# Row scales from squared rows of x, two projection pairs run alternately, and gate weights prepared early, in one hybrid mixer layer

## The chip, the cores and the metric

The kernel runs on one core of one Trainium2 chip. The metric is device time of one execution, in microseconds (us). The core's engines each work through their own instructions in order: TensorE (PE in the profile), VectorE (DVE), ScalarE (ACT), GpSimd (POOL) and SyncE (SP, which issues the DMAs). [...]

## The reference, cut to what matters

One layer, with 2048 tokens and 1024 channels. `w_in` has 8200 columns: q, k, v, the output gate, z_m, the i and f gates (4 columns each), u, B, C and z_c.

```python
h    = rms_norm(x, g_pre)                    # x * rsqrt(mean(x*x) + eps) * g_pre, per token
proj = einsum('bsd,de->bse', h, w_in)
q, k, v, o, z_m, i_pre, f_pre, u, gate_b, gate_c, z_c = split(proj)
hm   = mlstm_chunkwise(q*scale, k, v, i_pre + b_i, log_sigmoid(f_pre + b_f))   # 4 heads
y_m  = silu(z_m) * sigmoid(o) * group_rms_norm(hm, g_head, 4)
conv = causal_depthwise_conv(gate_c * u, conv_w)                               # 3 taps
y_c  = silu(z_c) * group_rms_norm(gate_b * conv, g_conv, 16)
out  = einsum('bse,ed->bsd', concat(y_m, y_c), w_out)
return x + rms_norm(out, g_post)
```

## The kernel before, in words

**Matmuls.** The inputs are float32, and PE multiplies in a rounded float32 format. So every operand is split into a rounded high part and the rest, its low part: a cast on ACT and a subtraction on DVE (`split_h`, `split_l`, L187 to L195). A product is then three matmuls per 128 rows of contraction: high by high, high by low, low by high (`mm_prod`, L300).

**Pairs and products.** The tokens are in two halves of 1024, each in two quarters of 512. The output columns of the projection are in 32 pairs of 128-column blocks (`PAIRS`). For one half of the tokens, a pair is a 2 by 2 block product (two column blocks, two token quarters, the contraction in two halves). It is done in the manner of Strassen and Winograd with 7 products instead of 8 (`pair`, L502). Each product is 12 matmuls of 512 columns into one of three banks of PSUM, X, D and Y. Between products the banks are copied or added on ACT and DVE (`evac`, L513): Y starts as a copy of X (L516), then p is copied from D (L519) and u2 from Y (L522). The token operands of the 7 products (hH and hL) are made once for a half, in seven sets j. The weight operands (w) are made for each product, some slots ahead (`plan_weights`, L294).

**Slots.** A slot is one product. An agenda (`on`, `later`, `run_slot`) holds what each slot emits behind its matmuls, sorted by level: evacuations, weights, stores, the rest. The order in which the program is written this way is kept on each engine (`in_order`), so nothing is reordered later. What falls into one slot stands in a row on its engine.

**The passes.** The opening (`start`, L918) loads x transposed, normalises the first half of the tokens, and does pairs 0 and 1 without Strassen, from operands that are not yet divided by the row's norm (uH, uL). The results are multiplied by the row's scale afterwards (`plain`, `plain_take`). Then come pairs 2 to 31 of the first half, 32 pairs of the second half, and two passes of the output projection with 16 pairs of 7 products each. Beside the pairs the agenda runs the gates (`plan_gates`), 32 groups of two chunks of mLSTM (`plan_group`, 16 for each half of the tokens), the convolution, and in the last pass the closing row norms (`row_take`, `row_rstd`, `row_out`).

**The opening's row scales.** ACT squares the 16 tiles of x transposed (L955). POOL adds them up over the channels (L960), a matmul by ones sums over the partitions and leaves the sum in every partition (`sum_up`, L964). ACT takes the root (L967) and DVE the reciprocal (L970): rb holds the scale of each token, in all partitions. With rb, `norm` scales x in place (L975), `diff` and `fill` make the 7 operand sets, and `plain_take` (L1017) scales the results of pairs 0 and 1. The gate projection (`gate_proj`, L558) takes weights wgt that `gate_weights` (L543) builds: a fill with zeros on DVE, two small casts on ACT, two small subtractions on DVE.

## Time and profile before

| | us |
|---|---|
| three runs, median (lowest to highest) | 1707.27 (1705.94 to 1707.9) |
| the profiled execution, its own time | 1707.94 |
| its span in the profile | 1706.2 |
| PE busy | 1653.8 (97%) |
| DVE busy | 1291.8 (76%) |
| ACT busy | 887.9 (52%) |
| POOL busy | 139.6 (8%) |

The mean granted clock of TensorE over the span is 0.987 of full speed. Below, a row of waits sums the idle time of an engine ahead of the instructions of one line, with the engine and line that ended it. A row of a timeline is one instruction, or several alike in a row ("x4", with their joint duration). Its bracket holds the engine's idle time just ahead of it and what ended that. Matmuls overlap in the pipeline, so their spacing, not their duration, is what each takes of PE's time.

### The profile page before, as it was taken

To read this page: it belongs to the slowest core of one execution; us is meant where nothing else is said; L and a number is where in the kernel's file an instruction comes from. 1 tells how busy PE (TensorE), PEld (TensorE's weight loads), DVE (VectorE), ACT (ScalarE), POOL (GpSimd) and SP (SyncE) were. 2 spreads that over 40 slices of the span, in tenths; PEclk is the share of its full clock that TensorE was granted. 3 is DMA by queue.
4 is the path that set the end of the run, shared out by engine and by line. 5 is a ranking of instruction groups with operands and counts; after the bars stand their busy time and mean duration, and the time that the engine had idled before them with its cause. 6 is when DMAs were issued, how large, how long until landed. Compare 5 with 4: busy or idle time off the path is not lost. (4 is left out here: it accounts for less than half of the span.)

```text
span 1706.2 us, 23384 instructions
## 1 busy us (share of the span) xinstructions
PE 1653.8 (97%) x7533; PEld 1368.6 (80%) x7533; DVE 1291.8 (76%) x2375; ACT 887.9 (52%) x1697; POOL 139.6 (8%) x152
## 2 busy tenths in 40 slices
PE   6789999999999999999999999999999999999997
PEld 4578888788888888778888888888888878887885
DVE  7887668788888798856556878686866685568886
ACT  6243446655655665634454556555655563355442
POOL 5000001010202000000000101010200000000110
PEclk9889999999999999999999999999999999999999
DMA  4177774546454788856876565556587788899774
GB/s 157 51 186 189 187 186 156 181 133 209 124 168 131 236 260 262 286 140 163 220 192 170 151 190 155 175 151 177 158 235 243 238 254 264 258 302 296 232 234 155
DMA packets 413389, 335.06 MB, mean 196 GB/s; under 512 B 191209, under 2 KB 305905, under 8 KB 413266
## 3 DMA queue, kind: packets, MB, share of 16 engines
q1 hardware_dynamic: 413266, 333.56, 66.0%
q8 instruction: 59, 0.97, 0.2%
q14 instruction: 64, 0.52, 0.1%
HBM read 214.71 MB, written 118.76 MB: 195 GB/s over the span
## 5 line engine op out<-in xcount | busy, mean ns | idle before, releaser
L188 ACT CAST w<-wraw 128x512 fp32r<-128x512 f32 x506 | 313.8, 622 | 278.6 <-PE uY L307 105.9
L191 DVE TENSOR_TENSOR w<-wraw,w 128x512 fp32r<-128x512 f32 x506 | 345.8, 686 | 120.0 <-ACT w L188 116.9
L305 PE MATMUL uY<-hH,w 128*128 128x512 f32 x936 | 368.3, 393 | 11.9 <-ACT uY L516 5.7
L306 PE MATMUL uY<-hL,w 128*128 128x512 f32 x936 | 365.7, 391 | 0.5 <-DVE hL L191 0.5
L307 PE MATMUL uY<-hH,w 128*128 128x512 f32 x936 | 366.2, 391 | 0.0
L305 PE MATMUL uX<-hH,w 128*128 128x512 f32 x624 | 245.5, 393 | 5.0 <-ACT w L188 5.0
L307 PE MATMUL uX<-hH,w 128*128 128x512 f32 x624 | 244.4, 392 | 4.2 <-DVE w L191 4.2
L305 PE MATMUL uD<-hH,w 128*128 128x512 f32 x624 | 244.5, 392 | 0.0
L306 PE MATMUL uX<-hL,w 128*128 128x512 f32 x624 | 244.0, 391 | 0.0
L307 PE MATMUL uD<-hH,w 128*128 128x512 f32 x624 | 243.6, 390 | 0.0
L306 PE MATMUL uD<-hL,w 128*128 128x512 f32 x624 | 243.3, 390 | 0.0
L305 PEld LDWEIGHTS uY<-hH,w 128*128 128x128 f32 x936 | 176.4, 188 | 51.2 <-ACT uY L516 7.5
L307 PEld LDWEIGHTS uY<-hH,w 128*128 128x128 f32 x936 | 176.2, 188 | 37.5
L306 PEld LDWEIGHTS uY<-hL,w 128*128 128x128 f32 x936 | 176.5, 189 | 36.6 <-DVE hL L191 1.1
L307 PEld LDWEIGHTS uX<-hH,w 128*128 128x128 f32 x624 | 117.7, 189 | 29.9 <-DVE w L191 4.9
L305 PEld LDWEIGHTS uX<-hH,w 128*128 128x128 f32 x624 | 117.8, 189 | 29.2 <-ACT w L188 5.5
L307 PEld LDWEIGHTS uD<-hH,w 128*128 128x128 f32 x624 | 117.2, 188 | 25.0
L306 PEld LDWEIGHTS uX<-hL,w 128*128 128x128 f32 x624 | 117.9, 189 | 24.0
L306 PEld LDWEIGHTS uD<-hL,w 128*128 128x128 f32 x624 | 117.4, 188 | 23.8
L305 PEld LDWEIGHTS uD<-hH,w 128*128 128x128 f32 x624 | 117.4, 188 | 23.5
L527 DVE TENSOR_TENSOR c<-p,uY 128x512 f32<-128x512 f32 x78 | 53.5, 686 | 93.0 <-PE uY L307 85.6
L421 POOL TENSOR_SCALAR hss<-hss 128x2 f32<-128x2 f32 x32 | 15.0, 470 | 1124.8 <-ACT num L790 1124.8
(198 smaller groups left out, 2275.7 us busy)
## 6 DMA issues: line engine op xcount, KB each, us to landing
wraw<-in_wt_dram SPq DMA_DIRECT2D x226, 256.0 KB
wraw<-w_scr SPq DMA_DIRECT2D x120, 256.0 KB
w_scr<-wraw SPq DMA_DIRECT2D x90, 256.0 KB
v_scr<-tr SPq DMA_DIRECT2D x128, 64.0 KB
vraw<-v_scr SPq DMA_DIRECT2D x32, 256.0 KB
h_scr<-hT SPq DMA_DIRECT2D x128, 64.0 KB
y_scr<-sg SPq DMA_DIRECT2D x32, 256.0 KB
g_scr<-c SPq DMA_DIRECT2D x32, 256.0 KB
```

The costliest lines, as they stand in the source:

```text
L188: nc.scalar.copy(dH, src)
L191: nc.vector.tensor_tensor(dL, src, dH.bitcast(F32), ALU.subtract)
L305: nc.tensor.matmul(bank, wH[:, k, :], bH[:, k, :], start=first, stop=False, **kw)
L306: nc.tensor.matmul(bank, wH[:, k, :], bL[:, k, :], start=False, stop=False, **kw)
L307: nc.tensor.matmul(bank, wL[:, k, :], bH[:, k, :], start=False, stop=stop and k == KH - 1, **kw)
L421: nc.gpsimd.tensor_scalar(t, t, scale, EPS, ALU.mult, ALU.add)
L527: nc.vector.tensor_tensor(c, sb["p"], bank["Y"], ALU.add)
```

## The change

**Row scales of the first half.** x is also loaded by rows (8 tiles of 128 tokens by 1024 channels, 512 KB each; `rows_load`). ACT squares a row tile and adds up along the row in the same instruction (`squares`, with accum_out). POOL turns four sums into four scales (`inverse`, by `rstd`: scale and eps, then the power -0.5, on 128x4). ACT multiplies the identity by each scale (`diagonal`), a matmul by ones spreads the diagonal over all partitions (`spread`), and ACT copies it to rb (`spread_take`). The squares of the transposed tiles, POOL's additions, ACT's roots and DVE's reciprocals are gone.

**Opening, other parts.** The gate weights' zero fill stands among the constants, and their load and splits stand ahead of the first slot's end. PE multiplies ones by zeros 16 times (128x128) before its first projection matmul. The two banks of pair 0's first quarter are copied to SBUF. The opening's steps stand in another order, set 1 is filled in the last slots ahead of pair 2, and sets 2, 4, 5 and 6 in the slots of pairs 2 and 3.

**Pairs 2 and 3.** Their 14 products run alternately (`two_pairs`, in the order TWO), pair 2's and 3's D banks in PSUM's pool "n".

**Groups, gates, last pass.** `plan_group` starts at slot 47 and every 10.4 slots (41 and 11 before), in the second half at U + 36 and every 10.8 (U + 34 and 11.3; U is the number of slots of a half). Within a group, q's scaling stands one slot later and in place, and its cast and subtraction one slot later. The steps of `plan_gates` from the row loads on stand one slot later, the takes of v of the opening 8 slots later. In the last pass `row_rstd` follows the second square at once instead of a slot later, and ot has 4 buffers instead of 5. The weights' raw tiles have 9 instead of 8.

The first place is ACT's order in the opening, from the end of the casts of pair 0's weights. Before (xs is x transposed, xsq its squares, w the weight operands, wgt the gate weights):

```order
L188 CAST w<-wraw 128x512 x2
L955 ACTIVATE xsq<-xs 128x512 x8
L188 CAST w<-wraw 128x512 x2
L947 ACTIVATE uH_172<-xs,gp 128x512 x4
L947 ACTIVATE uH_174<-xs,gp 128x512 x4
L967 ACTIVATE rb_167<-ssq,eps 128x512
L955 ACTIVATE xsq<-xs 128x512 x8
L188 CAST hH_430<-xs 128x1024 x2
L549 CAST wgt<-wgraw 128x8x4 x2
L564 COPY graw<-gate 100x512
```

After (xrows is x by rows, rs its sums of squares, dg the diagonal, graw the gate projection's result):

```order
L190 CAST w<-wraw 128x512 x4
L564 CAST wgt<-wgraw 128x8x4 x2
L1044 COPY u<-u 128x512 x2
L980 ACTIVATE xrows,rs_131<-xrows 128x1024 x4
L964 ACTIVATE uH_174<-xs,gp 128x512 x2
L989 ACTIVATE dg<-ident,rs_131 128x128 x4
L964 ACTIVATE uH_174<-xs,gp 128x512 x2
L964 ACTIVATE uH_176<-xs,gp 128x512 x4
L997 COPY rb_169<-ssq 128x512
L579 COPY graw<-gate 100x512
L980 ACTIVATE xrows,rs_131<-xrows 128x1024 x4
L989 ACTIVATE dg<-ident,rs_131 128x128 x4
```

The 16 squares of transposed tiles gave way to 8 squares of rows, four ahead of the second quarter's uH and four behind the first gate result. The gate weights' casts moved ahead of all of them.

The second place is ACT's order from the cast of a weight operand, ahead of and in pair 2. Before, pair 2 stands alone, and the hH in these rows are sets 5 and 6:

```order
L188 CAST w<-wraw 128x512
L188 CAST hH_676<-xs 128x1024 x2
L188 CAST w<-s_670 128x512
L188 CAST hH_688<-xs 128x1024
L188 CAST hH_688<-xs 128x512 x2
L188 CAST w<-wraw 128x512 x3
L516 COPY uY<-uX 128x512
L188 CAST w<-wraw 128x512
L519 COPY p<-uD 128x512
L188 CAST w<-wraw 128x512
L522 COPY u_811<-uY 128x512
```

After, in the slots of pairs 2 and 3, where cs, p and u are evacuations of both (hH_787 is set 4, hH_840 set 5, and u_859 is pair 2's u2):

```order
L190 CAST w<-wraw 128x512
L190 CAST hH_787<-xs 128x1024
L323 COPY cs<-uX 128x512
L190 CAST w<-wraw 128x512
L190 CAST hH_787<-xs 128x1024
L524 COPY p<-uD 128x512
L190 CAST w<-wraw 128x512
L190 CAST hH_840<-xs 128x1024
L527 COPY u_859<-uY 128x512
L190 CAST w<-wraw 128x512
L190 CAST hH_840<-xs 128x1024
```

Casts of sets 4 and 5 now stand between the evacuations.

The third place is the end of DVE's order, the last row tiles of the output (ot the row, oss its sums of squares, xr the rows of x). Before:

```order
L461 TENSOR_TENSOR ot<-uY,pc 128x512
L474 TENSOR_TENSOR ot<-ot,gpost 128x512 x2
L485 TENSOR_TENSOR oss<-oss 128x1
L493 SCALAR_TENSOR_TENSOR ot<-ot,oss,xr 128x512 x2
L474 TENSOR_TENSOR ot<-ot,gpost 128x512
L485 TENSOR_TENSOR oss<-oss 128x1
L493 SCALAR_TENSOR_TENSOR ot<-ot,oss,xr 128x512 x2
```

After:

```order
L465 TENSOR_TENSOR ot<-uY,pc 128x512
L489 TENSOR_TENSOR oss<-oss 128x1
L478 TENSOR_TENSOR ot<-ot,gpost 128x512 x2
L489 TENSOR_TENSOR oss<-oss 128x1
L497 SCALAR_TENSOR_TENSOR ot<-ot,oss,xr 128x512 x2
L478 TENSOR_TENSOR ot<-ot,gpost 128x512
L497 SCALAR_TENSOR_TENSOR ot<-ot,oss,xr 128x512 x2
```

The first sum moved ahead of two products by gpost. The second moved ahead of the first tile's two output instructions and of the last product by gpost, and with each sum the power on POOL that follows it.

The core of the diff:

```diff
+    rs0 = const.tile([P, NC], F32, name="rs0")
     wgt = const.tile([P, KT, GW], F32R, name="wgt")
+    nc.vector.tensor_copy(wgt.rearrange("p k f -> p (k f)"), zero[:, 0:1].broadcast_to([P, KT * GW]))
...
-    rawp = ctx.enter_context(tc.tile_pool(name="rawp", bufs=8))
+    rawp = ctx.enter_context(tc.tile_pool(name="rawp", bufs=9))
...
-    wseq = [(hf, n, j) for hf in range(2) for n in range(NPAIR) if (hf, n) not in ((0, 0), (0, 1))
-            for j in range(NPROD)]
+    TWO = [(0, 2 + c, j) for c, j in (
+        (0, 0), (1, 0), (0, 3), (1, 3), (0, 1), (0, 2), (1, 1), (0, 4), (1, 2), (0, 5), (1, 4), (0, 6), (1, 5), (1, 6))]
+    wseq = TWO + [(hf, n, j) for hf in range(2) for n in range(NPAIR) if hf or n > 3 for j in range(NPROD)]
...
-        o = S["ot", t, qd] = op.tile([P, Q], F32, tag="ot", name="ot", bufs=5)
+        o = S["ot", t, qd] = op.tile([P, Q], F32, tag="ot", name="ot", bufs=4)
...
-                later(0 if last else 1, lambda: row_rstd(t, last))
+                row_rstd(t, last)
...
-    def pair(hf, n):
-        bank = {"X": bank_("uX"), "D": bank_("uD")}
+    def products(hf, n, d_bank):
...
+        def step(j):
+            if j < 2:
+                bank["XD"[j]] = (bank_, d_bank)[j]("u" + "XD"[j])
+            mm_prod(bank["XDYXYDY"[j]], wops.pop((hf, n, j)), hops[hf, j], j < 2, True)
+            later(1, lambda: evac(j), EVAC)
+            run_slot()
+
+        return step
...
+    def two_pairs():
+        steps = {n: products(0, n, lambda name: ps.tile([P, Q], F32, tag="n", name=name, bufs=2)) for n in (2, 3)}
+        for _, n, j in TWO:
+            steps[n](j)
...
     def gate_weights():
-        raw = sm.tile([P, KT, 8], F32, tag="wgraw", name="wgraw", bufs=1)
-        nc.sync.dma_start(raw, wg)
-        nc.vector.tensor_copy(
-            wgt.rearrange("p k f -> p (k f)"), zero[:, 0:1].broadcast_to([P, KT * GW]))
+        raw = S.pop("wg")
...
-            st["tq"] = ml.tile([P, 2, P], F32, tag="tmp", name="tmp")
+            st["tq"] = q
             nc.vector.tensor_tensor(
                 st["kT"], st["kT"], st["R"][:, :, P - 1 : P].broadcast_to([P, 2, P]), ALU.mult)
-            nc.vector.scalar_tensor_tensor(st["tq"], q, SCALE, st["iw"], ALU.mult, ALU.mult)
...
             nc.vector.scalar_tensor_tensor(st["R"], st["sT"], SCALE, st["R"], ALU.mult, ALU.mult)
+            nc.vector.scalar_tensor_tensor(st["tq"], st["tq"], SCALE, st["iw"], ALU.mult, ALU.mult)
             high("k")
-            high("q")
...
         def lows():
             high("p")
+            high("q")
             low("k")
+
+        def more_lows():
+            low("p")
             low("q")
...
-        def unscaled(b, k):
+        def u_high(b, k):
+            nc.scalar.activation(U[b][0][:, k], raw(b, k)[:, 0], AF.Copy, scale=col(b, k))
+
+        def u_low(b, k):
...
-        ssq, acc = {}, {}
-
-        def square(b, k):
-            sq = t5("xsq")
-            nc.scalar.activation(sq, raw(b, k)[:, 0], AF.Square)
-            qd = b % 2
-            if qd not in acc:
-                acc[qd] = sq
-            else:
-                nc.gpsimd.tensor_tensor(acc[qd], acc[qd], sq, ALU.add)
-
-        def sum_up(qd):
+        xt_, ssq, dg = {}, {}, {}
+
+        def rows_load(i):
+            if i % 2 == 0:
+                xt_[i // 2] = hop_tile(i // 4, "HL"[i // 2 % 2], "xrows", F32)
+            nc.sync.dma_start(flat(xt_[i // 2])[:, i % 2 * DM : i % 2 * DM + DM], x[i * P : (i + 1) * P, :])
+
+        def squares(i):
+            t = flat(xt_[i // 2])[:, i % 2 * DM : i % 2 * DM + DM]
+            nc.scalar.activation(t, t, AF.Square, accum_out=rs0[:, i : i + 1])
+
+        def inverse(qd):
+            rstd(rs0[:, 4 * qd : 4 * qd + 4], 1.0 / DM)
+
+        def diagonal(qd):
+            dg[qd] = t5("dg")
+            for i in range(4):
+                c = 4 * qd + i
+                nc.scalar.activation(
+                    dg[qd][:, i * P : (i + 1) * P], ident, AF.Copy, scale=rs0[:, c : c + 1])
+
+        def spread(qd):
             ssq[qd] = ps.tile([P, Q], F32, tag="g", name="ssq")
-            nc.tensor.matmul(ssq[qd], ones, acc[qd], start=True, stop=True)
-
-        def root(qd):
-            nc.scalar.activation(rb[:, seg(qd)], ssq[qd], AF.Sqrt, bias=eps, scale=1.0 / DM)
-
-        def inverse(qd):
-            nc.vector.reciprocal(rb[:, seg(qd)], rb[:, seg(qd)])
+            nc.tensor.matmul(ssq[qd], ones, dg[qd], start=True, stop=True)
+
+        def spread_take(qd):
+            nc.scalar.copy(rb[:, seg(qd)], ssq[qd])
...
+        def fill(j, b, which=slice(None)):
+            if (0, j) not in hops:
+                hops[0, j] = hop_tile(j, "H", f"hH{j}"), hop_tile(j, "L", f"hL{j}")
+            H, L = hops[0, j]
+            for k, n in parts(b)[which]:
                 split(H[:, k : k + n], L[:, k : k + n], raw(b, k, n))
...
+        def plain_copy(bank):
             t = t5("u")
+            nc.scalar.copy(t, bank)
+            return t
...
-            slow = NSTART + 2 * ch + qd - clock[0] if kind == "v" else 0
+            slow = NSTART + 8 + 2 * ch + qd - clock[0] if kind == "v" else 0
...
+        S["wg"] = sm.tile([P, KT, 8], F32, tag="wgraw", name="wgraw", bufs=1)
+        nc.sync.dma_start(S["wg"], wg)
+        for i in range(4):
+            rows_load(i)
...
+        for i in range(4, NC):
+            rows_load(i)
...
+        warm = ps.tile([P, 2, P], F32, tag="s", name="warm")
+        for _ in range(16):
+            nc.tensor.matmul(warm[:, 0, :], ones, zero, start=True, stop=True)
...
-        weights(1, 0)
-        weights(1, 1)
-        for half in range(2):
-            for k in range(KH):
-                square(2 * half, k)
-        weights(1, 2)
-        weights(1, 3)
-        run_slot()
-        for b in (1, 3):
-            for k in range(KH):
-                unscaled(b, k)
-        p1 = [plain(1, 0, 0, lambda: sum_up(0))]
-        root(0)
+        for q in range(4):
+            weights(1, q)
+        gate_weights()
+        copies = [plain_copy(banks[ch]) for ch in range(2)]
+        for i in range(4):
+            squares(i)
         inverse(0)
-        norm(0)
-        for b in (1, 3):
-            for k in range(KH):
-                square(b, k)
-        run_slot()
-        p1.append(plain(1, 1, 0))
+        run_slot()
+
+        p1 = [plain(1, ch, 0) for ch in range(2)]
+        u_high(1, 0)
...
+        spread(0)
+        spread_take(0)
+        run_slot()
+
+        gate = gate_proj(((U[0], 0), (U[2], 1)))
...
+        gate_take(0, 0, gate)
+        norm(0)
+        for i in range(4, NC):
+            squares(i)
+        inverse(1)
...
+        diagonal(1)
+        fill(0, 0)
+        run_slot()
+
+        p0.append(plain(0, 1, 1))
+        spread(1)
+        fill(3, 2)
+        spread_take(1)
+        run_slot()
+
+        nc.sync.dma_start(r_scr.rearrange("(o t) -> o t", o=1), rb[0:1, :])
+        p1 = [plain(1, 0, 1)]
+        norm(1)
...
+        diff(0, 1, 0)
+        run_slot()
+
         gate = gate_proj(((U[1], 0), (U[3], 1)))
-        run_slot()
...
+        run_slot()
+        on(clock[0], lambda: fill(1, 1))
+        on(clock[0], lambda: gate_take(0, 1, gate))
+        run_slot()
+        on(clock[0], lambda: diff(1, 3, 0))
+        run_slot()
+        on(NSTART + 2, lambda: diff(2, 2, 1))
+        for i, (j, b, at) in enumerate(((2, 1, 0), (4, 0, 3), (5, 2, 5), (6, 3, 7))):
+            on(NSTART + at, lambda j=j, b=b: fill(j, b, slice(0, 1)))
+            on(NSTART + at + 1, lambda j=j, b=b: fill(j, b, slice(1, None)))
...
-    plan_gates(0, 15, True)
+    plan_gates(0, 18, True)
     plan_gates(1, U + 9, False)
     for i in range(NH * NG):
         h, g = divmod(i, NG)
-        plan_group(0, h, g, 41 + 11 * i)
-        plan_group(1, h, g, U + 34 + int(11.3 * i))
+        plan_group(0, h, g, 47 + int(10.4 * i))
+        plan_group(1, h, g, U + 36 + int(10.8 * i))
...
-    for n in range(2, NPAIR):
+    two_pairs()
+    for n in range(4, NPAIR):
```

## Rows read from the trace of the kernel before

**Rows 1.** The page's first part: busy us (share of span) xinstructions.
```profile
PE 1653.8 (97%) x7533; PEld 1368.6 (80%) x7533; DVE 1291.8 (76%) x2375; ACT 887.9 (52%) x1697; POOL 139.6 (8%) x152
```

**Rows 2.** Waits of PE, whole span: line waiting <- engine, line waited for: us, times, longest.
```profile
PE gate L558 <- DVE wgt L550: 8.9, 1, 8.9
PE u L1002 <- ACT w L188: 6.4, 1, 6.4
PE uY L305 <- ACT uY L516: 5.7, 4, 2.0
PE uX L305 <- ACT w L188: 5.0, 1, 5.0
PE uX L307 <- DVE w L191: 4.2, 1, 4.2
PE ssq L964 <- POOL xsq L960: 3.9, 1, 3.9
```

**Rows 3.** Windows: length, busy us per engine, granted clock, DMA share, GB/s.
```profile
80.00:100.00 20.00, 10.82 (x33) 7.82 (x32) 19.36 (x25) 13.14 (x19) 0.00 (x0) 0.66 0.46 133
...
300.00:310.00 10.00, 7.98 (x30) 6.31 (x29) 9.72 (x19) 7.58 (x14) 2.05 (x2) 0.83 0.48 178
```

**Rows 4.** Timeline of PE: start us, us, line, op, [idle before <-releaser].
```profile
47.65 0.75 PE L558 MATMUL gate<-uH,wgt 128*100 128x512 f32 x1 [8.89 <-DVE wgt L550]
...
53.63 1.02 PE L964 MATMUL ssq<-xsq,ones 128*128 128x512 f32 x2
...
54.72 0.40 PE L1003 MATMUL u<-uL,w 128*128 128x512 f32 x1
...
76.72 0.39 PE L558 MATMUL gate<-uH,wgt 128*100 128x512 f32 x1
...
85.59 0.79 PE L305 MATMUL uX<-hH,w 128*128 128x512 f32 x1 [5.02 <-ACT w L188]
```

**Rows 5.** DMA rate in 40 slices of 0 to 100 us.
```profile
GB/s 18 193 379 370 394 380 388 379 39 0 3 0 0 7 0 0 96 114 0 0 0 0 0 3 11 95 220 0 0 7 0 149 169 107 116 105 0 215 331 22
```

**Rows 6.** Timeline of DVE in the opening.
```profile
30.56 3.34 DVE L970 RECIPROCAL rb<-rb 128x512 f32<-128x512 f32 x1
33.93 6.47 DVE L975 SCALAR_TENSOR_TENSOR xs<-xs,gp,rb 128x512 f32<-128x512 f32 x4
...
41.52 2.72 DVE L975 SCALAR_TENSOR_TENSOR xs<-xs,gp,rb 128x512 f32<-128x512 f32 x4
44.17 2.35 DVE L191 TENSOR_TENSOR hL<-xs,hH 128x1024 fp32r<-128x1024 f32 x2
```

**Rows 7.** Timeline of ACT in the opening.
```profile
14.76 4.28 ACT L955 ACTIVATE xsq<-xs 128x512 f32<-128x512 f32 x8
...
19.97 5.01 ACT L947 ACTIVATE uH<-xs,gp 128x512 fp32r<-128x512 f32 x8
...
81.14 3.88 ACT L188 CAST hH<-xs 128x1024 fp32r<-128x1024 f32 x4
...
112.61 0.59 ACT L319 COPY cs<-uY 128x512 f32<-128x512 f32 x1 [2.10 <-PE uY L307]
...
131.65 0.59 ACT L319 COPY cs<-uY 128x512 f32<-128x512 f32 x1 [2.06 <-PE uY L307]
```

**Rows 8.** POOL by line: ns min/median/max, of the whole span.
```profile
L960 POOL TENSOR_TENSOR xsq<-xsq x14: 1282/1593/1632, 16.0 to 39.9; 128x512 f32<-128x512 f32 x14
...
L422 POOL TENSOR_TENSOR rs<-rs,mhalf x1: 1635/1635/1635, 466.9 to 466.9; 128x8 f32<-128x8 f32 x1
```

**Rows 9.** Timeline of ACT near 300 us.
```profile
293.68 1.06 ACT L822 ACTIVATE xn<-xn 128x1024 f32<-128x1024 f32 x1
...
301.33 1.28 ACT L343 ACT_TABLE_LOAD   x1
```

**Rows 10.** Timeline of DVE at the end.
```profile
1696.16 1.29 DVE L474 TENSOR_TENSOR ot<-ot,gpost 128x512 f32<-128x512 f32 x2 [0.84 <-ACT junk L465]
...
1701.62 1.41 DVE L493 SCALAR_TENSOR_TENSOR ot<-ot,oss,xr 128x512 f32<-128x512 f32 x2 [1.01 <-POOL oss L422]
```

More of the change, by code (lines that the diff above doesn't have):

```diff
@@ L500, in bank_ @@
         return pps.tile([P, Q], F32, tag="pp", name=name)
-    def pair(hf, n):
-        bank = {"X": bank_("uX"), "D": bank_("uD")}
+    def products(hf, n, d_bank):
+        bank = {}
         sb = {}
@@ L534, in evac, with pair @@
                 take(0, 1, bank["Y"], True)
-        for j in range(NPROD):
-            b = bank["XDYXYDY"[j]]
-            mm_prod(b, wops.pop((hf, n, j)), hops[hf, j], j < 2, True)
-            later(1, lambda j=j: evac(j), EVAC)
-            run_slot()
+        def step(j):
[5 more added lines that the diff above has]
+        return step
+    def pair(hf, n):
+        step = products(hf, n, bank_)
+        for j in range(NPROD):
+            step(j)
+    def two_pairs():
+        steps = {n: products(0, n, lambda name: ps.tile([P, Q], F32, tag="n", name=name, bufs=2)) for n in (2, 3)}
+        for _, n, j in TWO:
+            steps[n](j)
     def gate_weights():
-        raw = sm.tile([P, KT, 8], F32, tag="wgraw", name="wgraw", bufs=1)
-        nc.sync.dma_start(raw, wg)
-        nc.vector.tensor_copy(
-            wgt.rearrange("p k f -> p (k f)"), zero[:, 0:1].broadcast_to([P, KT * GW]))
+        raw = S.pop("wg")
         for w in range(2):
@@ L982, in diff @@
                 sub(raw(o, k, n), raw(a, k, n), raw(b, k, n))
-        def fill(j, b):
-            H, L = hops[0, j] = hop_tile(j, "H", f"hH{j}"), hop_tile(j, "L", f"hL{j}")
-            for k, n in parts(b):
+        def fill(j, b, which=slice(None)):
[3 more added lines that the diff above has]
+            for k, n in parts(b)[which]:
                 split(H[:, k : k + n], L[:, k : k + n], raw(b, k, n))
@@ L1004, in plain_k, with plain @@
             nc.tensor.matmul(bank, wL[:, k, :], bH[:, k, :], start=False, stop=end)
-        def plain(n, ch, qd, between=None):
+        def plain(n, ch, qd):
             bank = bank_("u")
@@ L1010, in plain, with plain_take @@
                     plain_k(bank, n, ch, qd, half, k)
-                if half == 0 and between:
-                    between()
             return bank
-        def plain_take(n, ch, qd, bank):
+        def plain_copy(bank):
             t = t5("u")
+            nc.scalar.copy(t, bank)
+            return t
+        def plain_take(n, ch, qd, bank, t=None):
+            t = t or t5("u")
             nc.vector.tensor_tensor(t, bank, rb[:, seg(qd)], ALU.mult)
             kind, i = PAIRS[n]
-            slow = NSTART + 2 * ch + qd - clock[0] if kind == "v" else 0
+            slow = NSTART + 8 + 2 * ch + qd - clock[0] if kind == "v" else 0
             later(slow, lambda: TAKE[kind](0, i, ch, qd, t, False))
@@ L1044, in start @@
             for k in range(KH):
-                unscaled(2 * half, k)
+                u_high(2 * half, k)
+                u_low(2 * half, k)
                 if k == 0:
@@ L1069, in start @@
-        run_slot()
-        p1.append(plain(1, 1, 0))
-        for ch in range(2):
-            plain_take(0, ch, 0, banks[ch])
-        norm(2)
-        fill(0, 0)
-        gate_weights()
+        for q in range(4):
[4 more added lines that the diff above has]
+            squares(i)
+        inverse(0)
+        run_slot()
+        p1 = [plain(1, ch, 0) for ch in range(2)]
+        u_high(1, 0)
+        u_high(1, 1)
@@ L1076, in start @@
+        diagonal(0)
+        u_high(1, 2)
+        u_high(1, 3)
+        for k in range(KH):
+            u_low(1, k)
+            u_high(3, k)
+            u_low(3, k)
+        spread(0)
+        spread_take(0)
         run_slot()
         gate = gate_proj(((U[0], 0), (U[2], 1)))
-        sum_up(1)
+        for ch in range(2):
+            plain_take(0, ch, 0, copies[ch], copies[ch])
+        for ch in range(2):
+            plain_take(1, ch, 0, p1[ch])
         gate_take(0, 0, gate)
-        root(1)
+        norm(0)
@@ L1086, in start @@
-        for ch in range(2):
-            plain_take(1, ch, 0, p1[ch])
         norm(3)
         run_slot()
-        p0.append(plain(0, 1, 1))
-        diff(0, 1, 0)
-        diff(1, 3, 1)
-        fill(1, 1)
-        run_slot()
-        p1 = [plain(1, 0, 1)]
-        fill(3, 2)
-        diff(1, 3, 0)
+        p1.append(plain(1, 1, 1))
         for ch in range(2):
```

21 lines of the change are left out of this document (6 added, 15 removed).

## The prediction

> **What bounds the kernel now.** The profile's first part comes first. PE is busy for 1653.8 us of a span of 1706.2, so some 52 us are all that waits can hold; DVE at 76% comes next [rows 1]. The waits of PE come second. Five of them, all in the opening, are 8.9, 6.4, 5.0, 4.2 and 3.9, together 28.4 [rows 2]. Later waits are small: behind the copy uY four times, 5.7 in all, 2.0 at most [rows 2].
>
> The windows show what a wait costs beside its idle time: from 80 to 100 us the granted clock was 0.66, from 300 to 310 it was 0.83 [rows 3]. [...]
>
> The opening in one sum: the last copy of pair 3 starts at 131.65 [rows 7]. Up to there PE has 224 projection and gate matmuls, 51.9 us at 0.2316, two ssq matmuls, some 0.86 each (53.63 to about 54.49, ahead of the row at 54.72 [rows 4]), 1.7, and 14 products. One product takes 19.04 / 7 = 2.72 between the copies at 112.61 and 131.65 [rows 7], so 14 take 38.1. With the first matmul at 6.4 [rows 2] that is 98.1. Lost are 33.5: the four later waits are 22.0, and 11.5 are the lower clock and late operands at the start. Of these 33.5, 13.1 fall into pairs 2 and 3: the second gate projection starts at 76.72 [rows 4], ends 16 x 0.23 later at 80.4, and 131.6 - 80.4 - 38.1 = 13.1.
>
> **The change part by part.** *Gate weights first.* The wait of 8.9 ends on DVE's last subtraction for wgt, behind DVE's queue of norms and hL up to 46.5 [rows 2, 6]. After, fill, casts and subtractions stand ahead of all that, by about 17. The wait and its 2.3 of lower clock go: -11.2.
>
> *Row scales.* The wait of 3.9 was for POOL's 14 additions at 1.6 [rows 2, 8]. They go. What must be in time now is ACT's chain to the diagonal. ACT's weight casts end by some 16: before, squares stood there from 14.76 at 0.53 each [rows 7]. Then come two bank copies to 19.4, when pair 0's first quarter is through PE, and four squares of rows at 1.06, the duration of the same instruction on xn [rows 9]: 23.7. Two uH (0.63 each [rows 7]) give 24.9. Meanwhile POOL does scale and power for 128x4. No row shows that shape: for 128x1 DVE waited 1.01 for both [rows 10], for 128x8 the power alone took 1.64 [rows 8], so 1.0 to 2.4. Four 128x128 multiplications by ACT are not shown either: below a bank copy of 0.59 each [rows 7] and above nothing, 0 to 2.4; I take 1.0, near a quarter of a uH plus a fixed part. The diagonal is ready at 26.5 to 27.2, at worst 28.7. PE needs it after 96 matmuls, at 29.7. So the wait goes to nothing with 1 to 3 us to spare. The second diagonal is ready at 42.2 and needed at 45.5.
>
> *New loads.* 8 x 512 KB are 4.2 MB, 11 us at the 380 GB/s of the opening's loads [rows 5]. Four rows stand ahead of the second quarter of x, which lands 5.5 later, by 26; its uH are issued from 23.7 to 30.4, and uL ends about 33, needed from 34. Hidden, with a us to spare. The other rows land by 31, needed at 34.7.
>
> *DVE in the opening.* It loses two reciprocals of 3.34, and its work beside POOL's additions gets shorter: norm x4 took 6.47 with POOL adding and 2.72 without [rows 6]. In all that is over 10 us of DVE time (6.7 + 3.8). None of it counts by itself; it is what lets sets 0, 1 and 3 be ready for pairs 2 and 3.
>
> *Start of PE.* The 16 multiplications of ones by zeros are quarters of an ssq matmul, 0.21 each at the higher clock, 0.43 at the lower. From 1.2 they end between 4.6 and 8.0; I take 7.1, later than the 6.4 of before, but with the clock up. DVE's first uL hold PE for 0.4 more by my replay. So the sum starts at 7.5, with bounds of 6.4 and 9; the lower clock of the start, a part of the 11.5 above, goes.
>
> *Pairs 2 and 3 alternately.* A product may now start while the other pair's evacuation runs, and the sets are wanted later: 2 and 4 in slots 6 to 8 instead of 2 to 4. ACT gets a queue, though: casts of hH at 0.97 [rows 7] stand between evacuations. Replaying both engines with the durations of before, pair 2's set 0 operand is 0.65 late; pair 2's fifth product waits for the copy u2, which stands behind a cast that DVE's sum releases at 78.8, then cast hH 1.0, p 0.5, cast w 0.5, cast hH 1.0, u2 0.5, at 82.9 instead of 81.1 (1.95 with the write); pair 3's u2 stands behind the gates' table load, 1.28 [rows 9], and costs 1.0. Together 3.6. Bounds: 0 and the 13.1 of before.
>
> The opening by the first paragraph's sum: 7.1 + 0.4 + 51.9 + 1.7 + 38.1 + 3.6 = 102.8 for the end of pair 3, instead of 131.6: -28.8.
>
> *Groups.* The wait of 2.0 at 303 us came in a slot in which ACT had a chunk's copy and square, a table load of 1.28 [rows 9], the next group's exponential, another table load and a sigmoid ahead of the copy uY; with the lower clock behind it (0.17 of 10 us [rows 3]) it cost 3.7. Such a queue stands ahead of a uY copy in two places of ACT's order before and in one after. But groups that come every 10.4 slots instead of 11 meet others elsewhere. I take -1.0, between -6 (all waits behind uY) and +4 (one more of this kind). The ninth raw tile and later takes move nothing on PE.
>
> *Last pass.* DVE's two waits of 1.01 for POOL's power, alike for both row tiles [rows 10], go, since each sum and power is issued one DVE instruction or more ahead of its use. Of these 2.0 I take 1.75, the sums themselves standing in the way; bounds 0 and -2.0.
>
> [...]
>
> Sum on the profiled execution, 1706.2 of span and 1.74 around it: 1707.94 - 28.8 - 1.0 - 1.75 = 1676.4. The median of the runs is 0.7 below that execution: 1675.7, so 1676.
>
> **The rivals.** *The alternation does not cover.* DVE was busy for 19.36 of 20 us from 80 to 100 [rows 3], so sums, hL and w come just in time, and one late uL or rb pushes all of it. The stalls grow from 3.6 toward the 13.1 of before: 9.5 more, 1685.5. Against it: DVE has over 10 us less ahead of this stretch.
>
> *All of it covers.* No stall in pairs 2 and 3 (-3.6), and the waits behind uY go with their clock (-5 more): 1667.5. For it: my replay of ACT has 0.1 of hand-off between instructions where slack may be; against it: the queue ahead of u2 is there in the order.
>
> *The scales come late, so the change does not do what it says.* The rows land late, or POOL's power is long, and PE waits for the spread as it did for POOL: as much as the removed gate wait, 8.9 + 2.3 less what is then ready in pairs 2 and 3, or 11: 1687. Against it: 1 to 3 us of slack at both places.
>
> *DVE held in the last pass.* In 16 row tiles the early sum waits up to 0.84, as the product by gpost did for ACT's square at 1696.16 [rows 10]; if all of it reaches PE, that is 13, and 1689. Against it: w is subtracted three slots, 8 us, ahead of its use.
>
> *Slower: denser groups.* The mechanism: ACT takes the next group's cast and exponential with two table loads in the slot that holds the previous group's second chunk, ahead of uY's copy. Each time costs the 3.7 of 303 us [rows 2, 3]. It decides from 9 of the 32 groups (33 against a gain of 31.6); at 16 it is 59 - 31.6 = 28 above before, 1735. For it: the spacing falls below the 11 slots that a group's two chunks and its lead span; against it: only one place of ACT's order has that row of instructions right ahead of uY.
>
> **How the numbers follow.** Forecast 1676: 0.52, with its own range of 1671 to 1682 (start, diagonal, groups and last pass at their bounds, not all the same way). Alternation does not cover, 1685.5: 0.21. All covers, 1667.5: 0.14. Scales late, 1687: 0.06. DVE held, 1689: 0.02. Denser groups, slower: 0.05. A measurement of this kernel can tell about 0.2%, 3.4 us, from no change; between 1704 and 1711 lies only the edge of the last case. Faster 0.94, same 0.01, slower 0.05. The range of 1667 to 1689 leaves out the slower case and the edges of the first two rivals.
>
> **What would show it right or wrong.** Right: no wait of gate for wgt and of ssq for its operand; a granted clock near 1.0 from 20 to 80; norm x4 of 2.7 throughout; the end of pair 3 at 102 to 104, with the longest waits there of uY behind u2; the last two ot at about 1701.6 - 28.8 - 1.0 - 1.75 = 1670. Wrong: a wait of the spread matmul for dg; a clock of 0.66 again around 60 to 90; more than two waits of 2 us behind uY between 130 and 1400; waits of products for w in the last pass. The forecast falls if the end of pair 3 lies beyond 108, or if PE's idle time after it grows by more than 4.

## The result

The changed kernel takes 1680.9 us (median of 4 runs, 1679.38 to 1682.57). The kernel before, on the same chip, takes 1707.59. The ratio is 0.9848, with a 95% interval of 0.9832 to 0.9863: 1.5% faster. The forecast was 1676, with an own range of 1671 to 1682.

The profiled execution took 1679.38 (span 1677.6), 28.6 less than that of before. It lies 1.5 below the median of its runs. The first part of the page and the waits of PE (line waiting <- engine, line waited for: us, times, longest), to be read against [rows 1, 2]:

```profile
PE 1648.6 (98%) x7565; PEld 1366.9 (81%) x7565; DVE 1276.7 (76%) x2373; ACT 885.2 (53%) x1703; POOL 129.5 (8%) x142
```

```profile
PE uY L309 <- DVE c L532: 6.3, 5, 3.0
PE uY L309 <- ACT u L527: 5.0, 2, 3.3
PE uX L309 <- ACT uY L521: 2.2, 2, 1.5
...
PE uX L311 <- DVE w L193: 1.6, 1, 1.6
```

Of the five waits of the opening, those for wgt, for the squares' sum and for ACT's w are gone, and so is the one ahead of the first projection, where PE now does the multiplications by zeros. The wait for DVE's w is 1.6 instead of 4.2. The largest sum is now on DVE's c, 6.3 in five waits, one of them 3.0. PE's timeline in the opening (start us, us, line and operation, [idle before <- releaser]) shows the order of events, against [rows 4]:

```profile
30.00 1.02 PE L994 MATMUL ssq<-dg,ones 128*128 128x512 f32 x2
...
45.54 1.02 PE L994 MATMUL ssq<-dg,ones 128*128 128x512 f32 x2
...
61.29 0.39 PE L309 MATMUL uX<-hH,w 128*128 128x512 f32 x1
...
63.49 0.50 PE L311 MATMUL uX<-hH,w 128*128 128x512 f32 x1 [1.58 <-DVE w L193]
...
70.26 0.50 PE L309 MATMUL uX<-hH,w 128*128 128x512 f32 x1 [1.50 <-ACT uY L521]
...
73.97 0.50 PE L309 MATMUL uX<-hH,w 128*128 128x512 f32 x1 [0.68 <-ACT uY L521]
...
104.27 0.39 PE L309 MATMUL uX<-hH,w 128*128 128x512 f32 x1
...
110.70 0.50 PE L309 MATMUL uY<-hH,w 128*128 128x512 f32 x1 [0.83 <-ACT uY L521]
...
124.92 0.50 PE L309 MATMUL uY<-hH,w 128*128 128x512 f32 x1 [3.05 <-DVE c L532]
...
127.78 0.39 PE L309 MATMUL uX<-hH,w 128*128 128x512 f32 x1
```

Both spread matmuls (30.00 and 45.54) run without a wait. Pairs 2 and 3 run from 61.29 to 104.27, where pair 4's first matmul stands. In the trace of before that matmul stands at 131.45:

```profile
131.45 0.39 PE L305 MATMUL uX<-hH,w 128*128 128x512 f32 x1
```

So the opening gave 27.2. Pair 5 starts at 127.78, 23.5 behind pair 4, where 19.04 are the rule [rows 7]: 4.5 are lost in pair 4.

The windows (length, busy us of each engine, granted clock, DMA share, GB/s), against [rows 3]:

```profile
60.00:80.00 20.00, 16.25 (x69) 12.30 (x68) 19.90 (x27) 10.47 (x15) 0.00 (x0) 1.00 0.44 133
80.00:100.00 20.00, 20.00 (x89) 16.29 (x88) 19.49 (x39) 13.08 (x21) 0.00 (x0) 1.00 0.57 153
300.00:310.00 10.00, 10.00 (x46) 8.25 (x45) 7.65 (x14) 5.13 (x12) 0.00 (x0) 1.00 0.79 223
```

The granted clock is 1.00 in all three. From 60 to 100 DVE is busy for 39.4 of 40 us, though.

From 104.27 on the account closes as follows. The last sum of uY and pc, at 1667.61, stands 1563.3 behind pair 4's start, against 1563.2 before. The loss of 4.5 in pair 4 is made up by 4.3 in the rest. PE's idle time from 200 us on fell from 12.2 to 10.0, and the stretch of lower clock behind 303 us (0.51 from 305 to 307 in the kernel before) is gone. From that last sum to the last outputs it takes 5.43 instead of 6.99 (1694.63 to 1701.62), against [rows 10]. DVE's end, in the trace of the change:

```profile
1667.61 0.69 DVE L465 TENSOR_TENSOR ot<-uY,pc 128x512 f32<-128x512 f32 x1 [0.63 <-PE uY L311]
...
1673.04 1.41 DVE L497 SCALAR_TENSOR_TENSOR ot<-ot,oss,xr 128x512 f32<-128x512 f32 x2
```

Together: -27.2 + 0.2 - 1.6 = -28.6.

### The profile page after: what moved, and what is told of

It reads as the page before. It is cut to its first block, busy times and chain, and to the rows that moved or that the text cites. A ratio compares the mean times of both kernels' runs of the same rounds, so it can differ in the third digit from the quotient of the medians.

```text
span 1677.6 us, 23360 instructions
## 1 busy us (share of the span) xinstructions
PE 1648.6 (98%) x7565; PEld 1366.9 (81%) x7565; DVE 1276.7 (76%) x2373; ACT 885.2 (53%) x1703; POOL 129.5 (8%) x142
## 5 line engine op out<-in xcount | busy, mean ns | idle before, releaser
L309 PEld LDWEIGHTS uD<-hH,w 128*128 128x128 f32 x624 | 117.2, 188 | 23.5
L527 ACT COPY u<-uY 128x512 f32<-128x512 f32 x78 | 45.6, 585 | 94.1 <-PE uY L311 92.8
```

What stands on the lines that cost most here:

```text
L309: nc.tensor.matmul(bank, wH[:, k, :], bH[:, k, :], start=first, stop=False, **kw)
L527: nc.scalar.copy(sb["u"], bank["Y"])
```

## The experiments

Each run is compared with the kernel before on its own chip. There the kernel before took 1706.6 to 1707.3 (three chips), so up to about 1 us of a difference between two runs can lie in the chips. The text of each expectation was fixed before the run.

**Gate weights first, alone, in the kernel before.**

```diff
+    nc.vector.tensor_copy(wgt.rearrange("p k f -> p (k f)"), zero[:, 0:1].broadcast_to([P, KT * GW]))
...
         nc.sync.dma_start(gb, gate_bias)
+        S["wg"] = sm.tile([P, KT, 8], F32, tag="wgraw", name="wgraw", bufs=1)
+        nc.sync.dma_start(S["wg"], wg)
...
         weights(1, 3)
+        gate_weights()
...
         fill(0, 0)
-        gate_weights()
```

> The kernel before, with one part of the change alone: the gate weights are filled, loaded and split ahead of the first slot's end. Theory A (the sum of the prediction): the wait of 8.9 us for wgt and 2.3 us of lower clock go, DVE's reciprocal for the second quarter moves up by about 9 as well, so nothing is late next: 1696 to 1697, and the last copy of pair 3 at about 120.5 instead of 131.65. Rival B (DVE's queue from 55 to 95 us is what really sets the start of pairs 2 and 3, and it does not move up): the waits for w in pair 2 grow by what the gate wait loses, 1703 or more, last copy of pair 3 at 127 or later.

Measured: 1698.84, ratio 0.9949 (0.9935 to 0.9964), 8.4 less than before. Pair 4 starts at 123.70, 7.8 earlier. PE in pairs 2 and 3 of this run:

```profile
83.02 0.80 PE L308 MATMUL uX<-hH,w 128*128 128x512 f32 x1 [6.63 <-DVE w L192]
```

The wait for wgt is gone, but the wait for DVE's w is 6.63 instead of 4.2 [rows 2], and a new one of 1.49 for DVE stands at 54.95. The result lies between the two theories: A's 11 shrink to 8.4, since PE next waits 2.5 to 4 longer for DVE.

**The old squares in the changed kernel.**

```diff
-            nc.scalar.activation(t, t, AF.Square, accum_out=rs0[:, i : i + 1])
...
+                nc.scalar.activation(sq, raw(b, k)[:, 0], AF.Square)
...
+                    nc.gpsimd.tensor_tensor(dg[qd], dg[qd], sq, ALU.add)
...
         def inverse(qd):
-            rstd(rs0[:, 4 * qd : 4 * qd + 4], 1.0 / DM)
+            nc.vector.reciprocal(rb[:, seg(qd)], rb[:, seg(qd)])
...
-            nc.scalar.copy(rb[:, seg(qd)], ssq[qd])
+            nc.scalar.activation(rb[:, seg(qd)], ssq[qd], AF.Sqrt, bias=eps, scale=1.0 / DM)
+            inverse(qd)
```

> The changed kernel with the old way to the row scales in the changed kernel's places: squares of the transposed tiles on ACT, sums on POOL, root on ACT, reciprocal on DVE; no rows of x are loaded. Theory A: POOL's seven additions at 1.6 us end at about 31.5 and 46.5, so the two spread matmuls wait 1 to 2 us each; two reciprocals (6.7 us) and slower norms (3.8 us) put DVE 10 us back, and DVE is just in time in pairs 2 and 3: waits there grow by 8 to 12. In all 1691 to 1695, end of pair 3 at 114 to 118. Rival B (DVE's lost time is covered, as only POOL's wait was on the path): 1683 to 1686, end of pair 3 at 106 to 109.

Measured: 1693.09, ratio 0.992 (0.9903 to 0.9937), 12.2 more than the change. Pair 4 starts at 115.12, 10.9 later. PE's timeline of this run:

```profile
31.77 0.70 PE L996 MATMUL ssq<-xsq,ones 128*128 128x512 f32 x1 [1.25 <-POOL xsq L986]
...
50.42 0.92 PE L996 MATMUL ssq<-xsq,ones 128*128 128x512 f32 x1 [2.83 <-POOL xsq L986]
...
74.31 0.80 PE L311 MATMUL uX<-hH,w 128*128 128x512 f32 x1 [5.83 <-DVE w L193]
```

Theory A has the time and the place of pair 4, but not the split. The two waits for POOL's sums are 1.25 and 2.83, and the waits in pairs 2 and 3 grew by 2.8 only: 5.83 for the first w, where the change has 1.58, and 0.69 for the copies, where it has 2.18. What decides is when DVE delivers that w. PE has it at 74.31 instead of 63.49, 10.8 later, and pair 4 starts as much later. DVE was busy without a gap from 40 to 60 us in this run (20.0 of 20), so PE's waits for POOL lie inside those 10.8. Of the parts that were run against the changed kernel, this is the largest.

**Pairs 2 and 3 in turn.**

```diff
...
-        for i, (j, b, at) in enumerate(((2, 1, 0), (4, 0, 3), (5, 2, 5), (6, 3, 7))):
+        for i, (j, b, at) in enumerate(((2, 1, 0), (4, 0, 2), (5, 2, 3), (6, 3, 4))):
...
-    two_pairs()
-    for n in range(4, NPAIR):
+    for n in range(2, NPAIR):
```

> The changed kernel with pairs 2 and 3 one after the other, as before, and the operand sets 4, 5 and 6 made one to three slots earlier, as that order needs them. Theory A (the alternation hides the making of the sets): waits in pairs 2 and 3 grow from 3.8 to about 13: 1688 to 1692. Rival B (the alternation only moves the waits: what it saves in pairs 2 and 3 comes back at 110 to 125 us, where two pairs' stores and evacuations fall together): the waits at 110.7 and 124.9 (0.8 and 3.0) vanish and pairs 2 and 3 lose about as much: 1680 to 1683.

Measured: 1683.4, ratio 0.9861 (0.9846 to 0.9876), 2.5 more than the change. Pair 4 starts at 110.85, 6.6 later; its waits in pairs 2 and 3 are nine small ones, 8.3 in all. No wait stands behind it up to 280 us. Pair 5 starts at 129.89, only 2.1 later than in the change. So most of what the alternation saves in pairs 2 and 3 is lost again in pair 4. Rival B has the mechanism. A rest of 2.5 stays; the intervals of the two ratios overlap, so its size is not firm.

**Without the 16 first multiplications.**

```diff
-        for _ in range(16):
-            nc.tensor.matmul(warm[:, 0, :], ones, zero, start=True, stop=True)
```

> The changed kernel without the 16 multiplications of ones by zeros. Theory A (the prediction's start): the first matmuls run at the lower clock again, 12 of them cost 2.4 us, of which 1 to 2 reach the end of the first projections: 1682 to 1683, end of pair 3 at 105.3 to 106.3. Rival B (DVE's chain of uL, norms and diff sets the start of pair 2, and PE waits there 1.58 for w anyway): the second gate projection ends 1 to 2 later, the wait of 1.58 shrinks by as much, end of pair 3 stays at 104.3 within 0.3: 1681.

Measured: 1680.59, ratio 0.9843 (0.9828 to 0.9858), the same as the change. The second gate projection ends 1.3 later, at 62.58; the wait for w shrinks from 1.58 to 1.09, the later one for c from 3.05 to 2.64. Pair 4 starts 0.8 later, pair 5 only 0.4. Rival B holds in the end, though the wait for w shrank by 0.5 where it had 1 to 2: what is won at PE's start is waited away behind DVE.

**Pair 1's takes later.** The trace of the change shows what precedes the wait of 3.05. DVE's timeline, then SP's (issues of DMAs):

```profile
119.33 0.69 DVE L251 TENSOR_TENSOR s<-wraw 128x512 f32<-128x512 f32 x1 [5.59 <-DMA wraw<-in_wt_dram]
...
124.22 0.65 DVE L532 TENSOR_TENSOR c<-p,uY 128x512 f32<-128x512 f32 x1
```

```profile
98.42 2.30 SPq L214 DMA_DIRECT2D v_scr<-tr  x4
...
101.84 2.12 SPq L214 DMA_DIRECT2D v_scr<-tr  x4
...
106.80 2.09 SPq L214 DMA_DIRECT2D v_scr<-tr  x4
108.99 0.45 SPq L244 DMA_DIRECT2D wraw<-in_wt_dram  x1
...
110.48 5.68 SPq L214 DMA_DIRECT2D v_scr<-tr  x8
116.21 0.50 SPq L244 DMA_DIRECT2D wraw<-in_wt_dram  x1
...
117.24 0.43 SPq L244 DMA_DIRECT2D wraw<-in_wt_dram  x1
```

The sum c at 124.22 stands behind a weight sum that waited 5.59 for a load (and, later, a scan of the gates that waited 0.88 for its row). SP issued weight loads only at 108.99, 116.21 and 117.24, behind stores of v and k of pairs 1 to 3, 0.5 to 0.7 us for each 64 KB (four in 2.1 to 2.3, eight in 5.7). The edit:

```diff
-            slow = NSTART + 8 + 2 * ch + qd - clock[0] if kind == "v" else 0
+            slow = NSTART + 13 + 2 * (2 * ch + qd) - clock[0] if kind == "v" else 0
```

> The changed kernel, in which the four takes of pair 1 (v, each a transposition and four stores of 64 KB) stand at slots 13, 15, 17 and 19 behind the opening instead of 8 to 11. Theory C (SP's queue: from 96 to 116 us SP issues the stores of pairs 1, 2 and 3 one behind the other, so the next weight loads are issued late, DVE waits 5.6 us for them and PE 0.8 and 3.0 behind DVE): the loads are issued 4 to 8 us earlier, both waits of PE go or fall below 1 together, 1677 to 1678. Rival D (DVE is late by the gates' scans, which stand ahead of pair 4's evacuation, whatever SP does): the wait at 124.9 stays at 2 or more, 1680 to 1681.

Measured: 1677.55, ratio 0.9831 (0.9816 to 0.9846), 3.4 less than the change. SP and PE of this run:

```profile
108.53 0.51 SPq L244 DMA_DIRECT2D wraw<-in_wt_dram  x1
...
109.65 0.43 SPq L244 DMA_DIRECT2D wraw<-in_wt_dram  x1
```

```profile
121.48 0.50 PE L309 MATMUL uY<-hH,w 128*128 128x512 f32 x1 [0.78 <-DVE c L532]
...
124.33 0.39 PE L309 MATMUL uX<-hH,w 128*128 128x512 f32 x1
```

The loads of 116.21 and 117.24 are issued at 108.53 and 109.65, and one wait of 0.78 is left. Pair 4 starts nearly as in the change (104.22), pair 5 at 124.33 instead of 127.78. Theory C holds.

**The old spacing of the groups.**

```diff
-        plan_group(0, h, g, 47 + int(10.4 * i))
-        plan_group(1, h, g, U + 36 + int(10.8 * i))
+        plan_group(0, h, g, 47 + 11 * i)
+        plan_group(1, h, g, U + 36 + int(11.3 * i))
```

> The changed kernel with the groups every 11 and 11.3 slots again (first at slot 47 and U + 36 as changed). Theory A (the denser spacing is worth about 1 us, as predicted): PE's idle time from 200 us on grows from 10.0 to 11 or 12, 1682 to 1683. Rival B (spacing only moves which evacuations a group meets; the waits of before, 2.0 and 1.7, went because q's scaling and casts stand a slot later): idle time stays within 1 of 10.0, 1680 to 1681.5. Rival C (denser was worse): 8 or less, 1677 to 1679.

Measured: 1685.58, ratio 0.9878 (0.9864 to 0.9893), 4.7 more than the change. PE's idle time from 200 us on is 13.4 instead of 10.0, and the wait of 2.0 of before is back:

```profile
365.74 0.80 PE L309 MATMUL uY<-hH,w 128*128 128x512 f32 x1 [2.02 <-ACT uY L521]
```

```profile
300.00:400.00 100.00, 97.98 (x453) 81.88 (x452) 81.68 (x162) 59.41 (x117) 11.46 (x10) 0.98 0.52 160
```

The clock falls again behind it (0.98 over these 100 us, with matmuls 0.43 apart from 366.33). A has the sign; the measured size is more than twice A's. Part of that may not belong to the spacing: in this execution pair 5 starts 25.8 behind pair 4 (23.5 in the change), as the granted clock fell to 0.50 behind a wait of 2.89 there. The edit does not move the first group, which stands at slot 47 in both and so behind pair 4. How much of this is in the median is not known. B falls: this run has q's steps a slot later, and the wait is there.

**The row sums a slot later.**

```diff
-                row_rstd(t, last)
+                later(0 if last else 1, lambda: row_rstd(t, last))
```

> The changed kernel with the sum of a row's squares a slot later again in the last pass (4 buffers for ot kept). Theory A (the prediction's last step): from the last sum of uY and pc to the last two outputs it takes 7.0 instead of 5.4, two waits of 1.0 for POOL are back: 1682.4. Rival B (first in, first out: the early sum holds DVE for ACT's squares in the 16 row tiles of the last pass, and that reaches PE): the tail loses 1.6 and the last pass gains as much or more, 1679 to 1681.

Measured: 1686.46, ratio 0.988 (0.9863 to 0.9896), with its runs from 1682.47 to 1689.13. PE's last wait of this run, and DVE's end:

```profile
1554.51 0.50 PE L309 MATMUL uY<-hH,w 128*128 128x512 f32 x1 [3.00 <-DVE c L532]
```

```profile
1677.34 1.42 DVE L497 SCALAR_TENSOR_TENSOR ot<-ot,oss,xr 128x512 f32<-128x512 f32 x2 [1.01 <-POOL oss L426]
...
1680.44 1.42 DVE L497 SCALAR_TENSOR_TENSOR ot<-ot,oss,xr 128x512 f32<-128x512 f32 x2 [1.01 <-POOL oss L426]
```

The end takes 7.00 again, from 1673.44 to 1680.44: A's 1.6 is shown. The time rose by 5.6, though. In this execution a wait for c in the last pass is 3.00, 0.60 in the change, and the clock falls behind it (0.97 from 1550 to 1600, 1.00 in the change); with four buffers a row held a slot longer may hold up the next sum, which was not tested. Another 1.6 are already lost when pair 5 starts, in pair 4, which the edit does not touch. Rival B finds no support, as nothing is gained in the pass. The late sum with five buffers was not tried, and how much of the last pass the fifth buffer is worth stays open. From 1523.34 to the last sum the change takes 144.3, the kernel before 143.2 (from 1551.41).

**Set 2 and the difference for set 1 later.** In pair 2 the product that adds to X waits for the copy of X to Y, and ACT does that copy behind casts of set 2.

```diff
         gate = gate_proj(((U[1], 0), (U[3], 1)))
-        diff(1, 3, 1)
...
+        on(clock[0], lambda: diff(1, 3, 1))
         on(clock[0], lambda: fill(1, 1))
...
-        for i, (j, b, at) in enumerate(((2, 1, 0), (4, 0, 3), (5, 2, 5), (6, 3, 7))):
+        for i, (j, b, at) in enumerate(((2, 1, 1), (4, 0, 3), (5, 2, 5), (6, 3, 7))):
```

> The changed kernel with set 2 filled one slot later (slots 1 and 2 of the two pairs) and the difference for set 1 three slots later, behind the low parts of the first w. Theory E (the three waits in pairs 2 and 3, 1.58, 1.50 and 0.68, come from what stands ahead in the queues: DVE's difference ahead of the first w's low part, ACT's casts of set 2, which wait for DVE, ahead of the copies of uX): all three go or sum to under 1, pair 4 starts at 101 to 102; if the waits of 0.8 and 3.0 behind it stay, 1677.5 to 1678.5. Rival F (DVE has no time left there: what goes ahead makes a set late): waits of products for hL in pairs 2 and 3 of 2 or more, pair 4 at 103.5 or later, 1680 to 1682.

Measured: 1682.56, ratio 0.9861 (0.9845 to 0.9878), with runs from 1677.51 to 1683.81.

```profile
68.34 0.50 PE L309 MATMUL uX<-hH,w 128*128 128x512 f32 x1 [1.38 <-ACT uY L521]
...
73.61 0.50 PE L309 MATMUL uX<-hH,w 128*128 128x512 f32 x1 [2.23 <-ACT uY L521]
...
104.38 0.39 PE L309 MATMUL uX<-hH,w 128*128 128x512 f32 x1
```

The wait of 1.58 is gone; in its place the two behind the copies are 1.38 and 2.23, together 1.4 more than before, and a new one of 0.36 came at 93. The sum is 4.0 instead of 3.8, and pair 4 starts at 104.38 instead of 104.27. E falls. F named a wait for hL that did not come, but its ground fits: the order changes, DVE's work does not, and the second copy now stands behind casts that wait for DVE's weight sum, as ACT shows:

```profile
71.51 0.62 ACT L190 CAST w<-wraw 128x512 fp32r<-128x512 f32 x1 [3.22 <-DVE wraw L251]
...
72.98 0.58 ACT L521 COPY uY<-uX 128x512 f32<-128x512 f32 x1
```

The profiled execution is the fastest of this run, at 1677.51; what the other three lost is in no trace.

**Work taken off DVE**, with the late takes of v kept. ACT copies pair 1's second quarter out of PSUM, and DVE multiplies it by the row scale 12 slots later.

```diff
-        plain_take(1, 0, 1, p1[0])
-        run_slot()
-        plain_take(1, 1, 1, p1[1])
-        run_slot()
+        for ch in range(2):
+            t = plain_copy(p1[ch])
+            on(NSTART + 12, lambda ch=ch, t=t: plain_take(1, ch, 1, t, t))
+            run_slot()
```

> The kernel of the late takes of v, with two more instructions taken off DVE ahead of pairs 2 and 3: pair 1's second quarter is copied out of PSUM by ACT, idle there, and DVE multiplies it by the row scale 12 slots behind the opening. Theory G (DVE is the bound from 48 to 80 us, so the waits of pairs 2 and 3 hang on the sum of DVE's work ahead and move when its order changes, but shrink when work leaves): 1.3 us less on DVE takes 1.0 to 1.3 off the waits of 3.3 in pairs 2 and 3, pair 4 starts at 102.9 to 103.2, 1676.3. Rival H (ACT's order sets them: the copies of uX stand behind ACT's casts whatever DVE does): pair 4 at 104.2, 1677.5.

Measured: 1676.35, ratio 0.9833 (0.9818 to 0.9848), with runs from 1675.1 to 1680.98. That is 1.2 less than with the late takes alone, but inside this spread; the trace carries the reading:

```profile
102.73 0.39 PE L309 MATMUL uX<-hH,w 128*128 128x512 f32 x1
```

Pair 4 starts there, 1.5 earlier than with the late takes alone (104.22); the waits ahead of it are 1.50 and 0.70, the 1.09 for w is gone. G holds, H does not.

**The gates two slots later as well.**

```diff
-    plan_gates(0, 18, True)
+    plan_gates(0, 20, True)
```

> As the run with ACT's copies and late multiplications, and the gates two slots later. Theory C (what is left at 121 us, 0.8, is DVE's wait of 2.5 for the gates' rows, issued late on SP behind eight stores of v): the rows land before the scan is due, the wait at 121 goes, 0.8 less than without the later gates, about 1675.5. Rival: the scans meet the next pair's evacuation in the same way and the wait moves there, no change.

Measured: 1674.24, ratio 0.9811 (0.9798 to 0.9825). The wait at 120 is gone, and PE waits for nothing from 72.41 to 271. This version beats both kernels: 6.7 less than the change, 33 less than before.

**And set 2 a slot later.**

```diff
-        for i, (j, b, at) in enumerate(((2, 1, 0), (4, 0, 3), (5, 2, 5), (6, 3, 7))):
+        for i, (j, b, at) in enumerate(((2, 1, 1), (4, 0, 3), (5, 2, 5), (6, 3, 7))):
```

> As the run with copies and later gates, and set 2 filled a slot later, so that on ACT the copies of uX stand ahead of the casts of set 2. Theory G (DVE is the bound): the waits keep their sum, pair 4 starts within 0.3 of the run without it. Rival H (ACT's order sets them): the waits of 1.5 and 0.7 go, pair 4 starts 1.5 to 2.2 earlier.

Measured: 1676.07, ratio 0.9823 (0.9809 to 0.9836). PE's timeline of this run:

```profile
72.63 0.50 PE L309 MATMUL uX<-hH,w 128*128 128x512 f32 x1 [2.23 <-ACT uY L521]
...
73.75 0.63 PE L309 MATMUL uX<-hH,w 128*128 128x512 f32 x1
...
75.88 0.63 PE L311 MATMUL uX<-hH,w 128*128 128x512 f32 x1
...
104.30 0.39 PE L309 MATMUL uX<-hH,w 128*128 128x512 f32 x1
```

One wait of 2.23 stands for 1.48 and 0.66: the sum is kept, as G has it. Yet pair 4 starts 1.8 later than in the run without this edit (102.51), where G had 0.3 at most. Behind the single wait the matmuls come 0.43 apart for some 3.5 us, with a granted clock of 0.66 from 72 to 77; behind the two shorter waits they come 0.23 apart, at 1.00 from 60 to 80.

## Why the prediction was right, point by point

- **Gate weights first.** The wait went, and the gate matmuls stand at 30.5, where the working had 30.6. Its "-11.2" is too much for this edit alone, which gave 8.4 in the kernel before: there PE waits 2.5 longer for DVE's w and 1.5 at a new place. Its 2.3 of lower clock follows from [rows 4]: from 47.65 to 53.63 the 16 gate matmuls took 5.98 at a granted clock of 0.60. At the spacing of 0.2316 from 54.72 to 76.72 (95 steps, granted clock 1.00), which the working also takes for its sums, they are 3.7.
- **Row scales.** The chain was read rightly. ACT and POOL in the changed kernel:

```profile
25.67 1.28 ACT L989 ACTIVATE dg<-ident,rs 128x128 f32<-128x128 f32 x4 [0.20 <-POOL rs L426]
...
42.45 1.28 ACT L989 ACTIVATE dg<-ident,rs 128x128 f32<-128x128 f32 x4 [2.95 <-POOL rs L426]
```

```profile
24.33 0.20 POOL L425 TENSOR_SCALAR rs<-rs 128x4 f32<-128x4 f32 x1 [22.69 <-ACT xrows L980]
24.61 1.03 POOL L426 TENSOR_TENSOR rs<-rs,mhalf 128x4 f32<-128x4 f32 x1
...
39.59 1.73 POOL L425 TENSOR_SCALAR rs<-rs 128x4 f32<-128x4 f32 x1 [13.95 <-ACT xrows L980]
41.40 1.02 POOL L426 TENSOR_TENSOR rs<-rs,mhalf 128x4 f32<-128x4 f32 x1
```

Scale and power together took 1.3 the first time, inside the bounds of 1.0 to 2.4, and 2.8 the second time, outside them: the power was the same, but the scale took 1.73 instead of 0.20. DVE was busy with its norms then and idle during the first scale; that this is the cause was not tested. Four multiplications by the identity took 1.28 (1.0 was taken). The diagonals end at 26.9 and 43.7, with 3.1 and 1.8 to spare, so neither reached PE. That DVE's saved time counts by itself at nothing but through the sets was right: the old squares cost 12.2, and the first w, which came 10.8 later from DVE, sets most of that.
- **New loads.** Hidden, as said: a row waited 0.37 for its DMA, once.
- **PE's start.** 6.5, forecast 7.1; the first spread matmul stands at 30.0, where the working had 29.7. No run shows the 0.21 and 0.43 taken for one multiplication by zeros: in the trace of the change one took 0.40 on average up to 4.79 us and 0.25 from there on. The lower clock of the start shows in the spacing alone, as the granted clock reads 1.00 from 6 to 20 us in the kernel before: there the matmuls come 0.43 apart from 7.02 to 11.33 and 0.23 apart from 11.64. In the change they come 0.23 apart from 9.58, and without the multiplications from 11.80. It did not matter: without the multiplications the time is the same.
- **Pairs 2 and 3.** 3.8 of waits, and 3.6 were forecast, but only the first place, pair 2's first product, was right, and there PE waited 1.58 for w's low part and not 0.65 for set 0. The two copies u2 cost nothing; the waits of 1.50 and 0.68 are for the copy of X to Y, ahead of the product that adds to X, which the forecast does not have. The right sum from mostly wrong places is luck. DVE was the bound there, and with it the sum holds while the place moves (runs with set 2 later); the forecast did not get its 3.6 from that.
- **The step that failed** is "The ninth raw tile and later takes move nothing on PE". The later takes put pair 1's stores of v among those of pairs 2 and 3, SP issued the weight loads behind them, and pair 4 lost 4.5; with the takes later still, pair 5 starts 3.5 earlier. It needs the alternation too: with the pairs in turn SP issues its loads about as late (108.33, 113.60 and 116.99), but pair 4 starts 6.6 later and nothing waits. This is the reason why the alternation is worth 2.5 in the end. What it is worth with the takes later still was not run, and the ninth raw tile was not run alone.
- **Groups.** Forecast -1.0, between -6 and +4. The rest of the kernel gave 4.3, and the old spacing costs 4.7, with the reserve above. The step was mis-sized: it took back most of the one wait it had found.
- **Last pass.** 1.56, forecast 1.75. The fourth rival's mechanism is in the trace, in small. DVE's sum of squares waits for ACT's square six times in the last pass (us in total, times, longest), where the kernel before has one wait for it, of 0.84, at the end [rows 10]:

```profile
DVE oss L489 <- ACT junk L469: 4.4, 6, 0.8
```

Five of these are 0.71 each, from 1576.89 to 1653.05, and PE has no wait in that stretch: they did not reach it. DVE's subtraction for w, next in its order behind the last of the five, starts only at 1653.13, though ACT's last cast of w ahead of it had ended at 1652.40.

None of the rivals' times came. The first one's ground did: DVE is just in time in pairs 2 and 3 (39.4 of 40 us). The 3.8 there go with it, as far as the run with work taken off DVE shows (1.1 of 3.3 went with two instructions, together 1.3 us); the 4.5 in pair 4 are SP's. Of the signs named for a right forecast, the two waits that should go, the full clock from 20 to 80 (1.00) and the short norms came; the end of pair 3 (104.3) missed its 102 to 104 by a little, the waits behind u2 did not come, and the last outputs stand at 1673.0 instead of 1670. On the profiled execution the forecast was a gain of 31.5 and 28.6 came: 1.6 less in the opening, 4.5 lost in pair 4, 3.3 more from the groups, 0.2 less at the end. The other 1.9 of the 4.9 between 1676 and 1680.9 is where the two profiled executions lie among their runs (0.4 above the median before, 1.5 below it after).

## What to carry to other kernels

When a change brings evacuations closer together, count what they issue on the engine that issues the DMAs, in order, with the time of each issue: here a load that stood behind twenty stores was issued over 7 us later than with fewer ahead of it. Where one engine is the bound over a stretch, expect another order to move the wait, and look for work to take off that engine: here two orders kept the sum of the waits (4.0 for 3.8, 2.2 for 2.1), and 1.3 us less work took 1.1 off 3.3. A gain ahead of such a stretch, as at PE's start here, is worth what the bound engine lets through.
